# A hybrid encoder layer on one core: the next head's decay mask queued behind the old head's last power, the first product's place fixed between the x tiles, and the first feed-forward products taken chunk by chunk

## The chip, the core and the metric

The kernel runs on one core of a Trainium2 chip. The core has a matrix engine (TensorE, PE in the profile; its weight loads are PEld), a vector engine (VectorE, DVE), an activation engine (ScalarE, ACT), a general engine (GpSimd, POOL) and a queue that issues transfers (SyncE, SP). Each has its own instruction queue and works through it in order; semaphores join them. The metric is the device time of one execution in microseconds (us), lower is better. A difference of the medians below 0.2% can't be told from no change.

## What is computed

One layer of a streaming encoder, on 1024 new frames of one stream and 64 next frames of another, 1088 tokens in all, width 1024:

```
z  = x @ w_in                                  # 1024 -> 8200 columns
A: GLU -> causal depthwise conv, width 31 -> LayerNorm -> swish -> @ w_a_out
B: 4 heads of a matrix memory, in chunks, gated with exp(d - m) below the diagonal
   h = num / max(|den|, exp(-m)); per-head norm (h - mu) * rsqrt(var + eps); sigmoid gate -> @ w_b_out
merged = sigmoid(g_A) * y_A + sigmoid(g_B) * y_B
x1 = LayerNorm(alpha * x + merged @ w_out)
x2 = LayerNorm(alpha * x1 + relu(x1 @ w_ff1)^2 @ w_ff2)       # hidden width 4096
```

All data are float32. Outputs are the two streams' x2 and the new states.

## The kernel before

**Products.** The 1088 tokens stand in three chunks of 384, 384 and 320 columns (`CHUNKS`), features on the 128 partitions. To keep float32 accuracy, every operand is split in a high part, rounded by ScalarE, and a low part, the difference, taken by VectorE (`split`, L339 and L342), and a product is three matmuls: high by high (L331), high by low (L334), low by high (L335), in `mm3`. A *unit* (`unit`) is 128 output features: eight k steps of three matmuls for each of three chunks, 72 matmuls, then a `post` function for each chunk, which evicts the PSUM tile. After each chunk `slot` advances background work by a step: the heads (`mlstm`), the convolution on VectorE (L572), and a third queue, misc, that holds the gates, the spilling of x and the norms. A unit's weights are loaded two units ahead (`wload`) and split one unit ahead (`wsplit`).

**Order.** A scheduler puts the instructions of each engine in order: those traced first have priority, but one whose operands its own model takes as ready may pass one that is not. `pin` sets an instruction behind the one traced before it on its engine; what comes after it may still pass. `tc.issue_after(i)` puts all that a block traces on the engine of `i` behind `i` in that engine's queue.

**Start.** x comes in nine tiles of 128 rows (`load_x`, L157, four buffers). `trans_x` transposes a tile on TensorE in two halves (L169), ScalarE takes the high part (L171), VectorE the low part (L172). Chunk 0 consists of tiles 0 to 2. Three tiles are asked for first, then the first weights, the fourth tile and the second weights. The first product, unit 0 on chunk 0, is traced after tile 2 and kept in `early` until its unit takes it. The gates (`gates`) ask for a few small transfers as well (L224, L225, L228).

**Heads.** Each of the four heads runs over nine chunks of 128 tokens. Chunk 8 is the second stream. At a chunk's end VectorE takes statistics of the head's output `isb` (L519 to L524), GpSimd computes the inverse root by an addition and a power (L525, L526), VectorE applies it (L527, L528), and TensorE transposes the result (L450) a step later. `head_decay` makes the next head's mask `dt`: GpSimd broadcasts a row (L391), fills (L392) and selects the part below the diagonal (L393), ScalarE takes nine exponentials (L395). `dt` has one buffer, so this can start when the old head has read its last mask (L478).

**First norm and feed-forward.** `out_proj` makes merged @ w_out chunk by chunk, eight products each, and starts `ln1` of a chunk when the chunk is done. `ln1` runs in the slots that follow: a split of the sum; then the mean over features (matmuls L697, L698), centred and squared data (L705, L707); then the variance (L716, L719) and a power; then the scale spread over the partitions (L730, L731), and `finish`, which leaves chunk `ci` of x1 as `X1H`, `X1L`, two feature blocks at a time (L820, L339, L342). The triple `waits` says how many slots pass ahead of the second, third and fourth of these steps. Then `first_units` takes the first two feed-forward units, each on chunks 0 and 1, then the third unit on chunks 0 and 1, kept in `early`, then both on chunk 2. The third unit's weights are the first in the pool `whl2`, whose space comes free at the end of `out_proj`. From there blocks of the feed-forward follow, in a seven-product scheme (`wino_pair`), then the last block and the second norm.

Of the kernel before, what the change touches and what calls it, by code (L numbers as in the profile page):

```python
# [20 lines left out]
T = SP + SS  # L21
P = 128
# [27 lines left out]
def hybrid_layer(ctx, tc, x_prompt, x_sample, cache_conv, state_C, state_n, state_m, w_in, b_gate,  # L50
# [36 lines left out]
    def gtile():  # L87
        return pools["psg"].tile([P, 512], F32, tag="m", name="g")
# [66 lines left out]
    def load_x(i):  # L155
        xt = xp.tile([P, D], F32, tag="x", name="x")
        nc.sync.dma_start(xt[:tile_len(i)], xrows(i))  # L157
        return xt

    def trans_x(i, xt):  # L160
        ci, off, n = i // 3, (i % 3) * P, tile_len(i)
        if i % 3 == 0:
            XH.append(ph.tile([P, KT, CN], F32R, tag="p", name="xh"))
            XL.append(pl.tile([P, KT, CN], F32R, tag="p", name="xl"))
        for kh in range(2):
            ps = mtile().rearrange("p (k t) -> p k t", k=4)
            for k in range(4):
                kk = kh * 4 + k
                TE.transpose(ps[:, k, :n], xt[:n, kk * P:(kk + 1) * P], ident[:n, :n])  # L169
            hi = XH[ci][:, kh * 4:kh * 4 + 4, off:off + n]  # L170
            S.activation(hi, ps[:, :, :n], AF.Copy)  # L171
            V.tensor_tensor(XL[ci][:, kh * 4:kh * 4 + 4, off:off + n], ps[:, :, :n], hi.bitcast(F32), ALU.subtract)  # L172

    xt0 = [load_x(0), load_x(1), load_x(2)]

    def start_x():
        for i in range(4):
            trans_x(i, xt0[i])
            if i == 1:
                wsplit(0, True)  # L180
            if i == 2:
                early[0] = product(*his[0], 0)
        for i in range(4, NT):
            trans_x(i, load_x(i))
        vp = xp.tile([NV, D], F32, tag="x", name="vp")
        nc.sync.dma_start(vp[0:CW, :], w_dw[0])
        for r, src in ((R_BDW, b_dw), (R_AG, ln_a_g), (R_AB, ln_a_b), (R_HN, hn_g), (R_G1, ln1_g), (R_B1, ln1_b)):
            nc.sync.dma_start(vp[r:r + 1, :], src[0:1, :])
        nc.sync.dma_start(vp[R_SN:R_SN + 1, :], state_n[0, 0].rearrange("h k -> (h k)")[None, :])
        cp = xp.tile([CB, D], F32, tag="x", name="cp")  # L190
        nc.sync.dma_start(cp, cache_conv[0, 0])
        ps = mtile()
        for k in range(KT):
            TE.transpose(ps[:, k * NV:(k + 1) * NV], vp[:, k * P:(k + 1) * P], ident[:NV, :NV])
        V.tensor_copy(vecs, ps[:, :KT * NV].rearrange("p (k v) -> p k v", k=KT))
        ps = mtile()
        for k in range(KT):
            TE.transpose(ps[:, k * CB:(k + 1) * CB], cp[:, k * P:(k + 1) * P], ident[:CB, :CB])
        V.tensor_copy(cacheT, ps[:, :KT * CB].rearrange("p (k v) -> p k v", k=KT))
# [115 lines left out]
    def product(hi, lo, ci):  # L315
        n = CHUNKS[ci][1]
        ps = gtile()
        for k in range(KT):
            mm3(ps[:, :n], hi[:, k, :], lo[:, k, :], XO["h"][ci][:, k, :n], XO["l"][ci][:, k, :n], k == 0, k == KT - 1)
        return ps  # L320

    def unit(hi, lo, post, chunks=(0, 1, 2)):
        for ci in chunks:
            ps = early.pop(ci) if ci in early else product(hi, lo, ci)
            while later:
                later.pop()()
            post(ci, *CHUNKS[ci], ps)
            slot()

    def mm3(out, lh, ll, rh, rl, start, stop, pinned=False, more=False):  # L330
        first = TE.matmul(out, lh, rh, start=start, stop=False, skip_group_check=more)  # L331
        if pinned:
            pin(first)
        TE.matmul(out, lh, rl, start=False, stop=False, skip_group_check=more)  # L334
        TE.matmul(out, ll, rh, start=False, stop=stop, skip_group_check=more)  # L335
# [39 lines left out]
    def head_start(h):  # L375
# [10 lines left out]
            G.memset(t[SS:, 8, :HD].bitcast(F32), 0.0)  # L386
        HT["vh"], HT["vl"] = vh, vl

    def head_decay(h):
        dt = pools["hd"].tile([P, NT, P], F32, tag="dt", name="dt")  # L390
        G.partition_broadcast(dt.rearrange("p c t -> p (c t)")[:, :T], negM[32 * h:32 * h + 1, :])  # L391
        G.memset(dt[:, 8, SS:], MASKED)  # L392
        G.affine_select(dt, dt, [[0, NT], [1, P]], ALU.is_ge, MASKED, base=0, channel_multiplier=-1)  # L393
        for c in range(NT):
            S.activation(dt[:, c, :], dt[:, c, :], AF.Exp, bias=ucol[:, c, h:h + 1])  # L395
        HT["dt"] = dt
# [29 lines left out]
    def mlstm(h):  # L426
# [30 lines left out]
        for c in range(NT):  # L457
# [65 lines left out]
            V.bn_aggr(st[:n, 10:12], st[:n, 4:10])  # L523
            V.tensor_scalar(st[:n, 2:3], st[:n, 11:12], st[:n, 1:2], st[:n, 1:2], ALU.mult, ALU.mult)  # L524
            G.tensor_scalar(st[:n, 3:4], st[:n, 2:3], EPS, None, ALU.add)  # L525
            G.tensor_tensor(st[:n, 12:13], st[:n, 3:4], mhalf[:n], ALU.pow)  # L526
            V.tensor_tensor(st[:n, 13:14], st[:n, 12:13], st[:n, 1:2], ALU.mult)  # L527
            V.tensor_scalar(isb[:n, :HD], isb[:n, :HD], st[:n, 10:11], st[:n, 13:14], ALU.subtract, ALU.mult)  # L528
            yield
# [286 lines left out]
    def ln1(ci):  # L816
        n = CHUNKS[ci][1]

        def finish(k, z):
            S.activation(z, z, AF.Identity, scale=vecs[:, k, R_G1:R_G1 + 1], bias=vecs[:, k, R_B1:R_B1 + 1])  # L820
            if k % 2:
                ks = slice(k - 1, k + 1)
                split(X1H[ci][:, ks, :n], X1L[ci][:, ks, :n], Y2[ci][:, ks, :n])
        X1H.append(ph.tile([P, KT, CN], F32R, tag="p", name="x1h"))
        X1L.append(pl.tile([P, KT, CN], F32R, tag="p", name="x1l"))

        def square():
            return pools["lnq" if ci == 2 else "ln1"].tile([P, 4, CN], F32, tag="sq", name="sq")
        yield from ln_feature(Y2[ci], n, pools["ln1"], square, finish, ((2, 3, 2), (2, 3, 2), (1, 2, 1))[ci], YS[ci])
        if ci == 2:  # L830
            lnq.close()
            lns.close()
            pools["hw0"] = pool("hw0", 1, stack=win)
# [166 lines left out]

    def first_units(kh, hi, lo):
        post = post_r(0, kh, True)
        unit(hi, lo, post, (0, 1))
        held.append((hi, lo, post))
        if kh == 1:
            pools["whl"] = pools["whl2"]
            third = 2 + next(i for i, p in enumerate(pieces) if p[3] == 1)
            wsplit(third)
            for ci in range(2):
                early[ci] = product(*his[third], ci)  # L1010
            drain("misc")
            for h in held:
                unit(*h, (2,))
            whs.close()
            pools["hw1"] = pool("hw1", 1, stack=win)
# [115 lines left out]
    def wload(i):  # L1131
        if i < len(pieces) and i not in raws:
            ap = pieces[i][0]
            raws[i] = wpool.tile([P, KT * P], F32, tag="wr", name="wr")
            nc.sync.dma_start(raws[i].rearrange("p (k n) -> p k n", n=int(ap.shape[2])), ap)
# [17 lines left out]

    idx = 0
    wload(0)
    xt0.append(load_x(3))
    wload(1)
    for ap, fn, kind, _ in jobs:
        if ap is None:
            fn()  # L1160
# [37 lines left out]
```

## Time and profile before

| | |
|---|---|
| timed runs before (3) | 1964.35, 1967.43, 1967.94 us; median 1967.43 |
| the profiled execution's own time | 1964.53 us |
| its span, first to last instruction | 1962.7 us |
| TensorE busy | 1930.5 us, 98% |
| VectorE, ScalarE, GpSimd busy | 1389.7 (71%), 637.7 (32%), 123.0 us (6%) |
| mean granted TensorE clock | 0.993 of full |
| bytes moved | 131.06 MB, mean 67 GB/s |

The profile is of one execution. A row of the timeline has the start, the length, the engine, the line, the operation, what is written and read, the count of merged instructions, and in brackets the idle time of the engine ahead of it with what ended it. A row of waits has the total idle time, the number of waits and the longest. A row of a table by stretches has the stretch, its length, then for PE, PEld, DVE, ACT and POOL the busy time and the number of instructions, the granted TensorE clock, the share of the 16 transfer engines and GB/s. Matmuls overlap, so a matmul's length is about twice the time from its start to the next one's.

### The profile page before, as it was taken

To read this page: it belongs to the slowest core of one execution; us is meant where nothing else is said; L and a number is where in the kernel's file an instruction comes from. 1 tells how busy PE (TensorE), PEld (TensorE's weight loads), DVE (VectorE), ACT (ScalarE), POOL (GpSimd) and SP (SyncE) were. 2 spreads that over 40 slices of the span, in tenths; PEclk is the share of its full clock that TensorE was granted. 3 is DMA by queue.
4 is the path that set the end of the run, shared out by engine and by line. 5 is a ranking of instruction groups with operands and counts; after the bars stand their busy time and mean duration, and the time that the engine had idled before them with its cause. 6 is when DMAs were issued, how large, how long until landed. Compare 5 with 4: busy or idle time off the path is not lost.

```text
span 1962.7 us, 30510 instructions
## 1 busy us (share of the span) xinstructions
PE 1930.5 (98%) x12396; PEld 1908.2 (97%) x12396; DVE 1389.7 (71%) x2735; ACT 637.7 (32%) x1203; POOL 123.0 (6%) x229
## 2 busy tenths in 40 slices
PE   8999999999999999999999998999999999999998
PEld 7999999999999999999999998999999999999996
DVE  3957876787678777887774547767685858577647
ACT  3323322332233223323352214523233332414232
POOL 1112210001000100000000000000000000000005
PEclk9999999999999999999999999999999999999999
DMA  4122311121212221225334211011111111111212
GB/s 152 37 82 54 120 49 55 54 71 48 62 35 65 64 66 34 65 89 181 119 107 146 91 39 39 22 54 33 54 44 54 44 44 55 44 55 34 75 44 91
DMA packets 171745, 131.06 MB, mean 67 GB/s; under 512 B 8272, under 2 KB 166464, under 8 KB 171604
## 3 DMA queue, kind: packets, MB, share of 16 engines
q1 hardware_dynamic: 171603, 129.11, 21.7%
q8 instruction: 97, 1.59, 0.3%
q14 instruction: 45, 0.36, 0.1%
HBM read 104.39 MB, written 24.63 MB: 66 GB/s over the span
## 4 chain that ended last, share of the span: by engine, by line
PE 91%; DVE 5%; issue 2%; POOL 1%; ACT 1%; DMA 0%; SPq 0%; DVEq 0%; POOLq 0%; ACTq 0%
PE g L331 28%; PE g L334 28%; PE g L335 28%; PE m L331 1%; PE m L335 1%; PE m L334 1%; DVE acc L572 1%; PE m L466 0%; PE m L1068 0%; PE m L413 0%; PE m L472 0%; DVE wl L342 0%; PE m L450 0%; DVE isb L528 0%; DVE C L504 0%
## 5 line engine op out<-in xcount | busy, mean ns | idle before, releaser
L331 PE MATMUL g<-xh,wh 128*128 128x384 f32 (+1 forms) x1920 | 636.0, 331 | 0.0
L334 PE MATMUL g<-xl,wh 128*128 128x384 f32 (+1 forms) x1920 | 630.8, 329 | 0.0
L335 PE MATMUL g<-xh,wl 128*128 128x384 f32 (+1 forms) x1920 | 629.8, 328 | 0.0
L334 PEld LDWEIGHTS g<-xl,wh 128*128 128x128 f32 x1920 | 362.6, 189 | 0.3
L331 PEld LDWEIGHTS g<-xh,wh 128*128 128x128 f32 x1920 | 362.5, 189 | 0.2
L335 PEld LDWEIGHTS g<-xh,wl 128*128 128x128 f32 x1920 | 362.2, 189 | 0.0
L572 DVE SCALAR_TENSOR_TENSOR acc<-glu,vecs,acc 128x1118 f32<-128x1118 f32 x240 | 331.4, 1381 | 3.5
L339 ACT ACTIVATE wh<-wr 128x1024 fp32r<-128x1024 f32 (+1 forms) x168 | 166.0, 988 | 458.4 <-PE g L334 363.6
L342 DVE TENSOR_TENSOR wl<-wr,wh 128x1024 fp32r<-128x1024 f32 (+1 forms) x168 | 191.1, 1138 | 113.6 <-ACT wh L339 110.8
L334 PE MATMUL g<-x1l,wh 128*128 128x384 f32 (+1 forms) x768 | 253.5, 330 | 1.6 <-DVE x1l L342 1.5
L331 PE MATMUL g<-x1h,wh 128*128 128x384 f32 (+1 forms) x768 | 254.3, 331 | 0.1
L335 PE MATMUL g<-x1h,wl 128*128 128x384 f32 (+1 forms) x768 | 253.0, 329 | 0.0
L334 PE MATMUL g<-hvl,wh 128*128 128x272 f32 x784 | 223.4, 287 | 0.0
L331 PE MATMUL g<-hvh,wh 128*128 128x272 f32 x784 | 221.3, 290 | 0.5 <-DVE y L981 0.5
L335 PE MATMUL g<-hvh,wl 128*128 128x272 f32 x784 | 221.6, 288 | 0.0
L983 DVE TENSOR_TENSOR y<-g,y 128x272 f32<-128x272 f32 (+1 forms) x540 | 156.6, 338 | 26.9 <-PE g L335 25.1
L331 PEld LDWEIGHTS g<-hvh,wh 128*128 128x128 f32 x784 | 145.8, 189 | 2.6 <-DVE y L983 1.3
L334 PEld LDWEIGHTS g<-x1l,wh 128*128 128x128 f32 x768 | 145.1, 189 | 2.4 <-DVE x1l L342 2.4
L334 PEld LDWEIGHTS g<-hvl,wh 128*128 128x128 f32 x784 | 147.3, 188 | 0.0
L335 PEld LDWEIGHTS g<-hvh,wl 128*128 128x128 f32 x784 | 146.4, 188 | 0.0
L331 PEld LDWEIGHTS g<-x1h,wh 128*128 128x128 f32 x768 | 145.1, 189 | 0.6 <-ACT x1h L339 0.5
L335 PEld LDWEIGHTS g<-x1h,wl 128*128 128x128 f32 x768 | 145.0, 189 | 0.0
(276 smaller groups left out, 2360.5 us busy)
## 6 DMA issues: line engine op xcount, KB each, us to landing
wr<-in_w_in_dram SPq DMA_DIRECT2D x64, 512.0 KB
wr<-in_w_ff_dram SPq DMA_DIRECT2D x64, 512.0 KB
x<-in_x_prompt_dram SPq DMA_DIRECT2D x8, 512.0 KB
dwT<-acc SPq DMA_DIRECT2D x8, 512.0 KB
wr<-in_w_b_out_dram SPq DMA_DIRECT2D x8, 512.0 KB
wr<-in_w_a_out_dram SPq DMA_DIRECT2D x8, 512.0 KB
wr<-in_w_out_dram SPq DMA_DIRECT2D x8, 512.0 KB
out_dram<-o SPq DMA_DIRECT2D x16, 256.0 KB
```

The costliest lines, as they stand in the source:

```text
L331: first = TE.matmul(out, lh, rh, start=start, stop=False, skip_group_check=more)
L334: TE.matmul(out, lh, rl, start=False, stop=False, skip_group_check=more)
L335: TE.matmul(out, ll, rh, start=False, stop=stop, skip_group_check=more)
L339: a = S.activation(hi, src, AF.Copy)
L342: V.tensor_tensor(lo, src, hi.bitcast(F32), ALU.subtract)
L572: V.scalar_tensor_tensor(acc, glu[:, j:j + AC], vecs[:, c, j:j + 1], acc, ALU.mult, ALU.add))
L983: V.tensor_tensor(y, ps[:, pslc], y, ALU.add)
```

## The change

Four edits. At the start, the first weights are asked for ahead of the first four tiles of x; the first product is pinned behind tile 3's transposes, tile 4's transposes stand pinned between its two halves of four k steps, tile 5's behind it, and the second weights are traced after tile 5's load. At the heads, the broadcast for the next head's mask is queued on GpSimd behind the last power traced so far, which is the old head's last one. In the first norm, chunk 1's steps pass (1, 3, 1) slots instead of (2, 3, 2). At the start of the feed-forward, the two first units are taken on chunk 0, then the third unit on chunk 0, then the two on chunk 1, the third on chunk 1, and then the two on chunk 2. The added test in `unit` keeps the kept products for the unit that takes all three chunks.

```diff
-    def trans_x(i, xt):
+    def trans_x(i, xt, pinned=False):
@@
-                TE.transpose(ps[:, k, :n], xt[:n, kk * P:(kk + 1) * P], ident[:n, :n])
+                t = TE.transpose(ps[:, k, :n], xt[:n, kk * P:(kk + 1) * P], ident[:n, :n])
+                if pinned and kk == 0:
+                    pin(t)
@@
-    xt0 = [load_x(0), load_x(1), load_x(2)]
+    xt0 = []
 
     def start_x():
-        for i in range(4):
+        for i in range(3):
             trans_x(i, xt0[i])
             if i == 1:
                 wsplit(0, True)
-            if i == 2:
-                early[0] = product(*his[0], 0)
-        for i in range(4, NT):
+        trans_x(3, xt0[3], True)
+        hi, lo = his[0]
+        ps = gtile()
+        for k in range(KT):
+            if k == KT // 2:
+                trans_x(4, load_x(4), True)
+            mm3(ps[:, :CN], hi[:, k, :], lo[:, k, :], XH[0][:, k, :], XL[0][:, k, :], k == 0, k == KT - 1, k % 4 == 0)
+        early[0] = ps
+        x5 = load_x(5)
+        wload(1)
+        trans_x(5, x5, True)
+        for i in range(6, NT):
             trans_x(i, load_x(i))
@@ unit
-            ps = early.pop(ci) if ci in early else product(hi, lo, ci)
+            ps = early.pop(ci) if ci in early and len(chunks) == 3 else product(hi, lo, ci)
@@ head_decay
-        G.partition_broadcast(dt.rearrange("p c t -> p (c t)")[:, :T], negM[32 * h:32 * h + 1, :])
+        with tc.issue_after(root[0].ins) if root[0] else ExitStack():
+            G.partition_broadcast(dt.rearrange("p c t -> p (c t)")[:, :T], negM[32 * h:32 * h + 1, :])
@@ mlstm
-            G.tensor_tensor(st[:n, 12:13], st[:n, 3:4], mhalf[:n], ALU.pow)
+            root[0] = G.tensor_tensor(st[:n, 12:13], st[:n, 3:4], mhalf[:n], ALU.pow)
@@ ln1
-        yield from ln_feature(Y2[ci], n, pools["ln1"], square, finish, ((2, 3, 2), (2, 3, 2), (1, 2, 1))[ci], YS[ci])
+        yield from ln_feature(Y2[ci], n, pools["ln1"], square, finish, ((2, 3, 2), (1, 3, 1), (1, 2, 1))[ci], YS[ci])
@@ first_units
-        unit(hi, lo, post, (0, 1))
+        unit(hi, lo, post, (0,))
         held.append((hi, lo, post))
         if kh == 1:
             pools["whl"] = pools["whl2"]
             third = 2 + next(i for i, p in enumerate(pieces) if p[3] == 1)
             wsplit(third)
-            for ci in range(2):
-                early[ci] = product(*his[third], ci)
+            early[0] = product(*his[third], 0)
+            for h in held:
+                unit(*h, (1,))
+            early[1] = product(*his[third], 1)
             drain("misc")
             for h in held:
                 unit(*h, (2,))
@@ start of the loop over jobs
     wload(0)
-    xt0.append(load_x(3))
-    wload(1)
+    for i in range(4):
+        xt0.append(load_x(i))
```

More of the change, by code (lines that the diff above doesn't have):

```diff
@@ L387, in head_start @@
         HT["vh"], HT["vl"] = vh, vl
+    root = [None]
     def head_decay(h):
         dt = pools["hd"].tile([P, NT, P], F32, tag="dt", name="dt")
-        G.partition_broadcast(dt.rearrange("p c t -> p (c t)")[:, :T], negM[32 * h:32 * h + 1, :])
+        with tc.issue_after(root[0].ins) if root[0] else ExitStack():
+            G.partition_broadcast(dt.rearrange("p c t -> p (c t)")[:, :T], negM[32 * h:32 * h + 1, :])
         G.memset(dt[:, 8, SS:], MASKED)
```

## The prediction

> **What bounds the kernel now.** I read the page first, then the list of TensorE's waits, then a table by stretches of the span round each wait.
>
> ```profile
> span 1962.7 us, 30510 instructions
> PE 1930.5 (98%) x12396; PEld 1908.2 (97%) x12396; DVE 1389.7 (71%) x2735; ACT 637.7 (32%) x1203; POOL 123.0 (6%) x229
> ...
> PE m L169 <- DMA x<-in_x_prompt_dram: 8.5, 3, 4.4
> PE m L450 <- DVE isb L528: 6.7, 3, 2.3
> PE m L716 <- ACT sh L339: 2.9, 1, 2.9
> PE g L334 <- DVE x1l L342: 1.5, 2, 1.0
> ```
>
> TensorE sets the time: busy 98%, and no other engine comes near. What can be won without removing products is its idle time. Four groups of waits hold nearly all of it: at the start (L169, loads of x), at the end of the heads (L450, one wait each for heads 0, 1 and 2), and at the end of the first norm (L716, L334). The change touches these three places. Behind them stands a second loss, in the clock column (the last three columns are granted clock, DMA share, GB/s):
>
> ```profile
> 10.90:17.80 6.90, 4.82 (x19) 4.40 (x20) 4.07 (x6) 3.23 (x6) 0.00 (x0) 0.51 0.99 321
> 254.00:258.00 4.00, 1.82 (x11) 1.43 (x11) 2.45 (x4) 1.00 (x1) 3.75 (x11) 1.00 0.30 93
> 464.00:480.00 16.00, 16.00 (x88) 16.00 (x89) 13.99 (x16) 3.70 (x10) 0.00 (x0) 0.89 0.01 3
> 672.00:690.00 18.00, 18.00 (x100) 18.00 (x100) 15.95 (x18) 3.59 (x9) 0.00 (x0) 0.91 0.10 26
> 1223.00:1231.00 8.00, 8.00 (x32) 8.00 (x33) 1.60 (x4) 0.52 (x1) 0.85 (x1) 0.59 0.14 47
> ```
>
> After the second and third head waits and after the norm's wait TensorE runs at half clock for a while, busy all through. Lost: 16 x 0.11 = 1.8, 18 x 0.09 = 1.6 and 8 x 0.41 = 3.3 us. After the first head's wait it does not.
>
> **The change part by part: heads.** The end of head 1, VectorE and GpSimd in order of time, with an ordinary chunk before it:
>
> ```profile
> 438.33 0.27 DVE L524 TENSOR_SCALAR st<-st 128x1 f32<-128x1 f32 x1
> 439.80 0.41 DVE L528 TENSOR_SCALAR isb<-isb,st 128x256 f32<-128x256 f32 x1
> ...
> 450.91 1.36 POOL L391 PARTITION_BROADCAST dt<-negM  x1 [6.08 <-DVE C L504]
> 452.43 0.26 DVE L524 TENSOR_SCALAR st<-st 64x1 f32<-64x1 f32 x1
> 459.51 1.22 DVE L342 TENSOR_TENSOR wl<-wr,wh 128x1024 fp32r<-128x1024 f32 x1 [6.81 <-ACT wh L339]
> 459.65 1.18 POOL L525 TENSOR_SCALAR st<-st 64x1 f32<-64x1 f32 x1 [6.67 <-issue]
> 461.38 0.59 POOL L526 TENSOR_TENSOR st<-st,mhalf 64x1 f32<-64x1 f32 x1
> 462.15 1.22 POOL L393 TENSOR_SCALAR_AFFINE_SELECT dt<-dt 128x1152 f32<-128x1152 f32 x1
> 462.19 1.32 DVE L528 TENSOR_SCALAR isb<-isb,st 64x256 f32<-64x256 f32 x1
> 463.40 2.74 ACT L395 ACTIVATE dt<-dt,cols 128x128 f32<-128x128 f32 x9 [2.31 <-POOL dt L393]
> ```
>
> In an ordinary chunk L528 ends 1.9 us after L524 starts. Here it ends 11.1 us after: the next head's broadcast went first, and 6.67 us of GpSimd follow in which nothing is recorded ("issue") before the addition L525 runs. With the broadcast queued behind the power, L525 to L528 keep their ordinary pace and isb is ready at about 454.4, against 463.51 now. Even if VectorE still takes the weight split at 459.51 first, L528 ends at 459.51 + 1.22 + 0.6 = 461.3, two us before it does now. The waits of 6.7 us go (bounds 6.7, and 6.0 in that second order), and with them the two half-clock stretches, 3.4 us. I take **10.1**.
>
> What now stands behind the power on GpSimd: code change, broadcast, mask selection L393, then on ScalarE the nine exponentials L395. The broadcast starts about 6.1 us (the idle time before it above) after L526 ends at 453.6, so 459.7; with 1.36, the fill L392 and 1.22 the mask is done at 462.5, and now it ends at 463.37. No later, so ScalarE is held no longer. The unrecorded 7 us move too, in front of the next arithmetic on GpSimd:
>
> ```profile
> 502.01 0.12 POOL L540 MEMSET glu<- 128x30 f32 x1 [38.64 <-DVE acc L572]
> 570.97 0.27 POOL L525 TENSOR_SCALAR st<-st 128x1 f32<-128x1 f32 x1 [68.84 <-DVE st L524]
> ```
>
> GpSimd stands idle for 68.84 us there, ample cover. If it were not hidden it would cost 6.67 at a power again, the present 2.3 us wait. The spills of x (L367), still running at the end of head 0, are delayed by some 7 us, and SP's queue with them; the weights queued behind them are for the unit after the next, three products of up to 4.2 us away. The Trainium skill, GPSIMD Engine Reference, 2.1 Instruction dispatch, says the first call of a freshly loaded kernel pays a load of about 6 us with no visible instruction; the rows agree (6.67 and 6.08). By that rule the change removes no load, it only moves them, and the sum stays as it is.
>
> **Start.** SP's queue, TensorE, and the two engines that feed the first product:
>
> ```profile
> 4.19 3.58 SPq L224 DMA_DIRECT2D fa<-in_w_in_dram  x1
> 10.68 2.65 SPq L157 DMA_DIRECT2D x<-in_x_prompt_dram  x4
> 13.87 1.96 SPq L228 DMA_DIRECT2D smc<-in_state_m_dram  x4
> ...
> 4.37 4.53 PE L169 MATMUL m<-ident,x 128*128 128x128 f32 x24 [4.37 <-DMA x<-in_x_prompt_dram]
> 11.03 1.94 PE L169 MATMUL m<-ident,x 128*128 128x128 f32 x8 [2.13 <-DMA x<-in_x_prompt_dram]
> 14.92 0.66 PE L169 MATMUL m<-ident,x 128*128 128x128 f32 x2 [1.95 <-DMA x<-in_x_prompt_dram]
> 15.23 0.67 PE L331 MATMUL g<-xh,wh 128*128 128x384 f32 x1
> 20.93 3.27 PE L169 MATMUL m<-ident,x 128*128 128x128 f32 x28
> ...
> 11.70 2.63 DVE L172 TENSOR_TENSOR xl<-m,xh 128x512 fp32r<-128x512 f32 x4
> ```
>
> Now x tile 3's transposes end at 12.97 and the operands are there by 13.0 (the first two of the four at 11.70), but the product waits behind tile 4, which lands at 14.9. After the change the first weights lead the queue. The four loads of x and the weights take 11.03 - 4.37 = 6.7 us from first to last landing, 1.65 each, so TensorE starts 1.6 us later, at 6.0; tile 3 still lands fifth, near 11. The product starts at about 13.1, half of it passes, then come tile 4's eight transposes and the other half. Now product and tile 4 are done at 20.93 + 4 x 0.117 = 21.4. Then: with the gaps of 2.13 and 1.95 gone the clock may be full, 13.1 + 4.2 + 0.9 = 18.3 (24 matmuls at 0.175, eight transposes at 0.117); at the half clock of this stretch, 13.1 + 3.8 + 1.9 + 2.1 = 20.9. If the four state loads (1.96 on SP) also pass tile 4, it lands at 16.9 and the end is 19.9 at full clock, 22.7 at half. So between 3.1 won and 1.3 lost; I take **2**, since the transposes follow one another nearly without gaps from 6.0 on. The second weights stay unpinned and are ready at once, so I expect SP to issue them ahead of tile 4 as before.
>
> **Norm's end.** The four products of the first two feed-forward units, and what follows:
>
> ```profile
> 1202.33 0.34 PE L730 MATMUL m<-sh,ones 128*128 128x384 f32 x1
> 1202.68 0.34 PE L331 MATMUL g<-x1h,wh 128*128 128x384 f32 x1
> 1206.86 0.31 PE L697 MATMUL m<-sh,mean 128*128 128x320 f32 x1
> 1212.37 1.23 DVE L342 TENSOR_TENSOR wl<-wr,wh 128x1024 fp32r<-128x1024 f32 x1 [0.59 <-ACT wh L339]
> 1222.79 0.37 PE L716 MATMUL m<-mean,sh 128*128 128x2 f32 x1 [2.88 <-ACT sh L339]
> 1230.82 0.31 PE L730 MATMUL m<-sh,ones 128*128 128x320 f32 x1
> 1234.17 0.83 DVE L342 TENSOR_TENSOR x1l<-y,x1h 128x640 fp32r<-128x640 f32 x1
> 1239.48 0.83 DVE L342 TENSOR_TENSOR x1l<-y,x1h 128x640 fp32r<-128x640 f32 x1 [0.50 <-ACT x1h L339]
> ```
>
> A product takes 1206.86 - 1202.68 = 4.18 us. From L730 of chunk 1 to L730 of chunk 2 are 28.5 us for four products (16.7) and some 1.3 us of norm matmuls: 10.5 are lost, idle or half clock (the norm's ten at 0.1 to 0.17 each). Afterwards chunk 1's norm steps stand one and two slots earlier in the output projection, and chunk 1 is first read after three products of chunk 0 instead of one, 8.4 us later. All the chunk-1 waits should go; L716 of chunk 2 stands behind four products instead of three and loses the stalls ahead of it, so its 2.88 and the half clock go as well. New: between chunk 2's L730 and the first product on chunk 2 stands one product, not two. Its low parts come 4.2 to 9.5 us after L730 (1235.0 to 1240.31), while the product on 320 columns starts at 4.5 (0.35 for L730 and L731, 4.18 for the one product) and would have done three quarters of its 3.5 us (4.18 x 320/384) when it asks for the last of them: TensorE waits up to 9.5 - 4.5 - 2.6 = 2.4 us. I take 2 for it, and 0.5 for the earlier L716 of chunk 1, which finds VectorE busy. Net **8.0**; bounds 10.5 (no new wait) and 3 (the third unit's weights, split at 1212.37 to 1213.6, are wanted from about 1211: 2.6, with chunk 2's wait 2.4 and a half-clock stretch 1.7 to 3).
>
> **Sum.** 10.1 + 2 + 8.0 = 20 us off the profiled execution's 1964.5 (span 1962.7): 1944.5. The three timed runs before have a median of 1967.4, 2.9 above the profiled one. I put the time at **1945**, near the profiled basis, since waits that may or may not draw a half-clock stretch are what goes.
>
> **Rivals.** (1) The norm's end wins little, as at the bound of 3: it then gives 3 and not 8, 1949.5, or nothing, 1952.5. For it: VectorE and ScalarE are nearly full from 1203 on; against: they get 7 us more lead. (2) The half clock is not due to the head waits: then the heads give 6.7 and the time is 1948. For it: the first head's wait of 2.3 us left the clock at 1.00; against: 0.89 and 0.91 directly after the other two. By the Trainium skill, TensorE: Matmul & The Clock Gate, What's actually happening, half rate comes after an idle window of about 3.4 us, longer than these waits, which would speak for this rival; the trace shows half clock after 2.3 us, so the measurement decides. (3) The change does not do what it says: the scheduler keeps its order at the heads through another queue (VectorE still behind a late split), and only start and norm pay: 1954. (4) Slower: the exponentials L395 are queued on ScalarE ahead of the evictions that follow the head's last chunk. ScalarE then stands from about where the broadcast starts now, 450.9, until 462.5 + 2.74 = 465.2, 14.3 us. Of the three PSUM buffers one is still being read when that begins, so two products, 8.4 us, are covered. TensorE stops for 5.9 us and loses 1.7 to 3.4 more to the clock: 7.6 to 9.3 for each of three heads, 23 to 28 in all, giving 1967.5 to 1972.5, say 1970. It turns slower than before from 20 / 3 = 6.7 per head. Against: the mask selection ends no later than now, and now the exponentials stand behind the evictions.
>
> **How the numbers follow.** Forecast (1939 to 1950) 0.70; rival 1 0.12; rival 2 0.04; rival 3 0.06; rival 4 0.04; something that cancels most of it, within 0.2% of before, 0.04. Less than 0.2% (3.9 us) cannot be told from no change here. Faster: 0.70 + 0.12 + 0.04 + 0.06 = 0.92, less 0.02 for their upper ends, 0.90; same 0.06; slower 0.04. The range: all three parts at their good end, 10.1 + 3.1 + 10.5 = 23.7, so 1940.8, and 1.8 for scatter, 1939; at the other side rivals 1 and 3 on the basis of the median, 1956. Left out: some 0.12.
>
> **What would show it.** Heads right: no wait of L450 on L528, L525 within 1 us of L524 at each head's end, broadcast after L526, clock 1.00 at 464 and 672; wrong: L450 or another wait of 2 us there, or ScalarE idle before L395 for over 5 us with TensorE waiting. Start right: the first L331 near 13 and the last of the product with tile 4 by 20; wrong: a wait for x in its middle. Norm right: no wait at L716, a wait of about 2 us at chunk 2's L334 instead; wrong: waits at the third unit's L335 on wl. The whole is wrong if TensorE's idle time falls and the time does not.

## The result and the profile after

The changed kernel takes 1945.8 us (median of four runs, 1944.61 to 1947.92), the kernel before on the same chip 1967.5 (four runs, 1964.35 to 1967.94). The ratio is 0.9894, with an interval of 0.9877 to 0.9911: 17.5 to 24.2 us less. The forecast was 1945. The profiled execution took 1945.67 us, with a span of 1943.9. Of the kernel with chunk 1's slots back, below, one execution of five (2565.99 us, granted clock 0.685 against 0.998 in the others) is left out of every figure.

The page of the changed kernel, its first lines, and then its list of TensorE's waits (total, number, longest):

```profile
span 1943.9 us, 30514 instructions
PE 1922.5 (99%) x12396; PEld 1902.4 (98%) x12396; DVE 1390.9 (72%) x2735; ACT 638.1 (33%) x1204; POOL 124.0 (6%) x229
...
PE m L169 <- DMA x<-in_x_prompt_dram: 6.9, 1, 6.9
PE g L342 <- DVE y L995: 1.5, 2, 1.2
...
PE g L345 <- DVE xl L174: 0.9, 1, 0.9
PE m L744 <- ACT sh L350: 0.8, 1, 0.8
```

The three waits for isb (6.7 us before) are gone from the list, and so are the norm's 2.9 and 1.5. Three loads' waits (8.5 us) have become one of 6.9. One wait has grown: for y at L995 (L981 before), which stood at 0.5. Two are new: for xl (0.9), and for sh at L744 (0.8). Line numbers of the changed kernel are up to 16 higher than before.

For the gain by stages, the same three matmuls in both timelines will do as marks: the gates' transposes, the last head's last transposes, and the first transposes of the second norm. The timeline of the kernel before, and then that of the changed kernel:

```profile
76.17 1.17 PE L308 MATMUL m<-ident,fa 128*128 128x128 f32 x9 [0.52 <-DMA fa<-fc]
870.56 0.34 PE L450 MATMUL m<-ident,isb 64*128 64x64 f32 x2
1851.81 1.04 PE L1068 MATMUL m<-ident,y 128*128 128x128 f32 x8
```

```profile
74.28 1.17 PE L319 MATMUL m<-ident,fa 128*128 128x128 f32 x9 [0.51 <-DMA fa<-fc]
858.67 0.34 PE L464 MATMUL m<-ident,isb 64*128 64x64 f32 x2
1832.59 1.04 PE L1084 MATMUL m<-ident,y 128*128 128x128 f32 x8
```

The start gives 76.17 - 74.28 = 1.9 us. From there to the last head it is 794.39 against 784.39: 10.0. From there to the second norm it is 981.25 against 973.92: 7.3. The rest takes 0.4 more. The same differences, worked out from the same three marks in every profile of this study (us; a part marked * holds the change's own edits of that stage and no others):

| kernel | start | heads | norm and feed-forward |
|---|---|---|---|
| before | 76.2 | 794.4 | 981.2 |
| after | 74.3 * | 784.4 * | 973.9 * |
| heads alone (e1) | 77.6 | 784.5 * | 981.3 |
| start alone (e2) | 74.1 * | 794.9 | 979.7 |
| norm alone (e3) | 77.2 | 796.3 | 972.4 * |
| broadcast by transfer (e6) | 78.0 | 786.8 | 981.3 |
| slots back (e4) | 76.3 * | 784.4 * | 975.4 |
| loads back (e5) | 75.5 | 784.4 * | 972.5 * |
| sums on GpSimd (e7) | 75.1 * | 784.4 * | 978.2 |
| split first (e8) | 74.2 | 784.4 * | 972.5 * |
| squares on ScalarE (e9) | 75.1 * | 784.4 * | 970.9 |
| start and squares (e11) | 74.0 | 784.4 * | 970.9 |

The start scatters by up to 2 us with the same code (74.1 to 76.3 with the change, 76.2 to 77.6 without; the 78.0 of e6 has a small transfer of its own there). Part of that is the clock: the profile with 76.3 (e4) has it at 0.91 from 30 to 50, 1.8 us, where the changed kernel has 1.00. The heads scatter hardly at all once their waits are gone.

The end of head 1 after, on VectorE, GpSimd and ScalarE:

```profile
448.36 0.27 DVE L538 TENSOR_SCALAR st<-st 64x1 f32<-64x1 f32 x1
449.80 0.41 DVE L542 TENSOR_SCALAR isb<-isb,st 64x256 f32<-64x256 f32 x1
455.91 2.02 DVE L353 TENSOR_TENSOR wl<-wr,wh 128x1024 fp32r<-128x1024 f32 x1 [1.31 <-ACT wh L350]
...
448.72 0.21 POOL L539 TENSOR_SCALAR st<-st 64x1 f32<-64x1 f32 x1 [0.74 <-DVE st L538]
449.02 0.56 POOL L540 TENSOR_TENSOR st<-st,mhalf 64x1 f32<-64x1 f32 x1
455.63 1.37 POOL L405 PARTITION_BROADCAST dt<-negM  x1 [6.06 <-issue]
457.08 1.94 POOL L407 TENSOR_SCALAR_AFFINE_SELECT dt<-dt 128x1152 f32<-128x1152 f32 x1
...
562.97 0.26 POOL L539 TENSOR_SCALAR st<-st 128x1 f32<-128x1 f32 x1 [68.82 <-DVE st L538]
...
459.05 2.75 ACT L409 ACTIVATE dt<-dt,cols 128x128 f32<-128x128 f32 x9 [1.54 <-POOL dt L407]
```

L538 to the end of L542 now takes 1.85 us, the pace of an ordinary chunk, where it took 11.1. The broadcast starts 6.05 us after the power's end. If the second unrecorded stretch is still there, it lies in GpSimd's idle time: the next addition, L539 at 562.97, has 68.82 us of idle time ahead of it and starts 0.11 us after its L538 ends (562.86).

### The profile page after: what moved, and what is told of

It is laid out like the page before. It is cut to its first block, busy times and chain, and to the rows that moved or that the text cites. A ratio compares the mean times of both kernels' runs of the same rounds, so it can differ in the third digit from the quotient of the medians.

```text
span 1943.9 us, 30514 instructions
## 1 busy us (share of the span) xinstructions
PE 1922.5 (99%) x12396; PEld 1902.4 (98%) x12396; DVE 1390.9 (72%) x2735; ACT 638.1 (33%) x1204; POOL 124.0 (6%) x229
## 4 chain that ended last, share of the span: by engine, by line
PE 94%; DVE 4%; DMA 1%; ACT 0%; issue 0%; POOL 0%; DVEq 0%; SPq 0%; POOLq 0%; ACTq 0%
PE g L342 29%; PE g L345 29%; PE g L346 29%; PE m L342 1%; PE m L346 1%; PE m L345 1%; DVE acc L586 1%; PE m L480 0%; PE m L1084 0%; PE m L427 0%; DVE wl L353 0%; PE m L486 0%; PE m L464 0%; DMA x<-in_x_prompt_dram 0%; PE m L169 0%
## 5 line engine op out<-in xcount | busy, mean ns | idle before, releaser
L342 PE MATMUL g<-xh,wh 128*128 128x384 f32 (+1 forms) x1920 | 634.9, 331 | 0.0
L346 PE MATMUL g<-xh,wl 128*128 128x384 f32 (+1 forms) x1920 | 628.6, 327 | 0.0
L342 PEld LDWEIGHTS g<-xh,wh 128*128 128x128 f32 x1920 | 361.3, 188 | 0.7 <-ACT xh L173 0.3
L346 PEld LDWEIGHTS g<-xh,wl 128*128 128x128 f32 x1920 | 361.0, 188 | 0.1
L342 PE MATMUL g<-x1h,wh 128*128 128x384 f32 (+1 forms) x768 | 252.8, 330 | 0.0
L346 PE MATMUL g<-x1h,wl 128*128 128x384 f32 (+1 forms) x768 | 252.1, 328 | 0.0
L342 PE MATMUL g<-hvh,wh 128*128 128x272 f32 x784 | 221.8, 291 | 1.5 <-DVE y L995 1.5
L346 PE MATMUL g<-hvh,wl 128*128 128x272 f32 x784 | 222.4, 289 | 0.0
L342 PEld LDWEIGHTS g<-hvh,wh 128*128 128x128 f32 x784 | 146.5, 190 | 3.4 <-DVE y L995 1.9
L346 PEld LDWEIGHTS g<-hvh,wl 128*128 128x128 f32 x784 | 147.1, 189 | 0.0
L342 PEld LDWEIGHTS g<-x1h,wh 128*128 128x128 f32 x768 | 144.2, 188 | 0.1
L346 PEld LDWEIGHTS g<-x1h,wl 128*128 128x128 f32 x768 | 144.3, 188 | 0.0
```

## The experiments

All times are compared with runs of the kernel before on the same chip. The first four ran beside it at a median of 1966.31 us, the next four at 1965.21, the last three at 1966.89. The changed kernel's own runs stand beside the 1967.51 above, not beside these. So where a kernel differs from it by less than 0.2% (3.9 us) and the intervals of the two ratios overlap, the medians don't decide, and the text goes by the stages of the profiles, one execution each.

**The heads alone (e1).** To the kernel before is added only:

```diff
+    root = [None]
+        with tc.issue_after(root[0].ins) if root[0] else ExitStack():
+            G.partition_broadcast(...)
-            G.tensor_tensor(st[:n, 12:13], ...)
+            root[0] = G.tensor_tensor(st[:n, 12:13], ...)
```

> The kernel before with one edit of the change alone: the broadcast queued behind the old head's last power. Theory A (order: the waits of TensorE at the three heads and the half-clock stretches behind two of them both go): 10 us less than before, about 1957, the granted clock 1.00 in the 30 us after each head's end, no wait of L450 on isb. Rival (the half clock has another cause and stays): 6.7 us less, and 0.89 to 0.91 still recorded in two stretches. Rival (other edits of the change are needed for it): no gain.

Measured: 1955.65 us, 10.7 less; ratio 0.9943 (0.993 to 0.9957). The stage of the heads shrinks by 9.9 us, and no wait for isb is left. A table by stretches of this kernel (busy PE, PEld, DVE, ACT, POOL with counts, clock, DMA share, GB/s):

```profile
464.00:480.00 16.00, 16.00 (x100) 16.00 (x99) 14.57 (x14) 3.19 (x7) 0.00 (x0) 1.00 0.17 45
672.00:690.00 18.00, 18.00 (x112) 18.00 (x111) 14.69 (x14) 3.44 (x5) 0.00 (x0) 1.00 0.14 35
```

The clock is 1.00 in the stretches that stood at 0.89 and 0.91. The rival by which the half clock stays (6.7) is out: the half clock went with the waits.

**The start alone (e2).** The kernel before with `trans_x`, `start_x` and the load order of the change.

> The kernel before with the edits of the start alone (order of the first loads and the pins). Theory A: 2 us less than before, about 1965.5 against 1967.5; TensorE's first transposes near 6.9, the product with tile 4 done near 19. Rival (the later start eats what the pins win): no difference. The trace of after gives 1.9 by the place of the gates' first transposes.

Measured: 1962.66 us (11 runs), 3.7 less; ratio 0.9985 (0.9976 to 0.9994), that is 1.2 to 4.7 us. Its timeline on TensorE:

```profile
6.79 5.96 PE L169 MATMUL m<-ident,x 128*128 128x128 f32 x32 [6.79 <-DMA x<-in_x_prompt_dram]
...
18.91 3.32 PE L169 MATMUL m<-ident,x 128*128 128x128 f32 x28
```

Product and tile 4 are done at 18.9, against 21.4 before. Over the five profiles with this start and the three with the old one (the table's first column: 74.3, 74.1, 76.3, 75.1, 75.1; 76.2, 77.6, 77.2) the mean gain is 77.0 - 75.0 = 2.0. In the profiled execution a part of the gain isn't the start's: the norm's wait was 1.4 us where the kernel before shows 2.9, and the stage is 1.5 shorter with the same code. So 2 us from the start agree with all of it; the rival (no gain) is out by the interval, though 3.7 us is just under 0.2%.

**The norm's end alone (e3).** The kernel before with `first_units`, the added test in `unit` and chunk 1's (1, 3, 1).

> The kernel before with the edits of the norm's end alone (the slots of chunk 1, the units by chunks). Theory A: 7 to 8 us less than before, about 1960; no wait at L716 and no half clock near 1223 to 1231, a wait of about 1.5 at the first seven-product block and half clock for some 3 us behind it. Rival (the gain at this place comes from the earlier parts, which shift the work against it): under 3 us.

Measured: 1958.74 us, 7.6 less; ratio 0.996 (0.9947 to 0.9972). The stage is 8.8 us shorter here, 1.5 more than in the changed kernel. The expected half clock at the first seven-product block didn't come: TensorE is busy for 8.51 of 10 us there (1258 to 1268), as in the changed kernel, but at a clock of 1.00 and not 0.83. The three medians add up to 10.7 + 3.7 + 7.6 = 22 us against 21.7 for all edits together: no sign that the parts disturb one another.

This kernel keeps the old heads, so its three head waits can be laid beside those of the two others that have them. In the kernel before, half clock followed the second and the third wait, not the first. The stretches behind the three waits in the kernel with the start alone:

```profile
254.00:266.00 12.00, 10.30 (x54) 10.23 (x55) 9.95 (x12) 2.74 (x9) 5.61 (x11) 0.86 0.29 86
462.00:474.00 12.00, 10.54 (x64) 10.47 (x65) 11.44 (x14) 3.64 (x10) 1.22 (x1) 1.00 0.16 42
668.00:680.00 12.00, 10.13 (x52) 10.06 (x53) 10.08 (x12) 2.74 (x9) 1.60 (x3) 0.86 0.18 45
```

and in this one:

```profile
254.00:266.00 12.00, 9.53 (x47) 9.14 (x46) 8.62 (x10) 4.86 (x12) 7.38 (x13) 0.86 0.29 85
462.00:474.00 12.00, 9.73 (x48) 9.35 (x47) 8.81 (x10) 4.79 (x12) 2.73 (x7) 0.86 0.18 45
668.00:680.00 12.00, 9.73 (x49) 9.35 (x48) 8.30 (x10) 5.41 (x12) 3.33 (x7) 0.86 0.18 45
```

Nearly the same wait (2.2 to 2.5 us) is followed by a half clock (0.86 over 12 us, 1.7 us lost) in some executions and not in others: seven times of nine. That fits the 1.9 us that the heads take longer here than in the kernel before (796.3 against 794.4): three stretches of half clock, not two.

**The broadcast by a transfer (e6).** The kernel before; the order at the heads is left, the code change is taken away:

```diff
+        nc.sync.dma_start(nmD, negM[0:P:32])
-        G.partition_broadcast(dt.rearrange(...)[:, :T], negM[32 * h:32 * h + 1, :])
+        nc.sync.dma_start(dt.rearrange(...)[:, :T], nmD[h:h + 1, :].partition_broadcast(P))
```

> The kernel before, with the order of the heads kept and the code change taken away: the rows of the decay mask are written to DRAM once, and each head's mask is filled by a broadcasting transfer on SP's queue instead of the broadcast on GpSimd. Theory A refined (the late addition is late because the broadcast ahead of it brings some 7 us of unrecorded time on GpSimd before the next arithmetic): the addition L525 follows its L524 within 1 us although the mask's order is untouched, no wait of L450, 10 us less than before, about 1957. Rival B (it is the order on GpSimd itself, the mask's fill and selection ahead of the addition): the addition still runs several us late, and the gain is under 5 us. Rival C (the transfer waits at the head of SP's queue and holds up the weights behind it): new waits of TensorE on weights, slower than the kernel with the broadcast alone moved.

Measured: 1957.33 us, 9.0 less; ratio 0.9951 (0.9938 to 0.9963). GpSimd at the end of head 1, and VectorE's L526, which is L524 of the kernel before:

```profile
453.61 1.21 POOL L395 TENSOR_SCALAR_AFFINE_SELECT dt<-dt 128x1152 f32<-128x1152 f32 x1 [0.46 <-DMA dt<-nmD]
...
454.91 0.21 POOL L527 TENSOR_SCALAR st<-st 64x1 f32<-64x1 f32 x1
...
453.78 0.27 DVE L526 TENSOR_SCALAR st<-st 64x1 f32<-64x1 f32 x1
```

The addition starts 0.86 us after L526 ends, although the mask's selection still stands ahead of it: without the broadcast there are no 6.67 unrecorded us. So what made the addition late was the broadcast ahead of it; that it is a load of code, as the prediction reads it, no run here shows. The order itself is not free: GpSimd stops at the selection for 0.46 us until the transfer has landed, and the addition behind it starts 0.86 us after its L526 where the changed kernel has 0.09. TensorE waits 2.0 us for isb in this kernel, 1.6 of it at head 0. Most of the lateness there is not the order's: VectorE's step behind the power, L529, takes 1.64 us at head 0 and 0.15 at head 1, while GpSimd adds up x for its spills beside it. The list of waits, and head 0 on VectorE and GpSimd:

```profile
PE m L452 <- DVE isb L530: 2.0, 2, 1.6
```

```profile
248.76 1.64 DVE L529 TENSOR_TENSOR st<-st 64x1 f32<-64x1 f32 x1 [1.71 <-POOL st L528]
...
248.70 1.68 POOL L369 TENSOR_TENSOR xs<-xh,xl 128x320 f32<-128x320 f32 x2
```

The profile's stage of the heads is 7.6 us shorter against 9.9 with the broadcast moved, and a half clock follows the wait at head 0 (0.92 from 240 to 262). Theory A refined holds for the mechanism and was 1 to 2.5 us too good on the size; of rival B the 0.86 us remain, and of rival C nothing shows.

**Chunk 1's slots back (e4).**

```diff
-((2, 3, 2), (1, 3, 1), (1, 2, 1))[ci]
+((2, 3, 2), (2, 3, 2), (1, 2, 1))[ci]
```

> The changed kernel with chunk 1's slots back at (2, 3, 2), the order of the units by chunks kept. Theory A (both halves of the edit are needed: the order gives chunk 1 two products more, the slots give its steps two places more): chunk 1 of x1 comes two slots later, some 8 us, and TensorE waits for it at its first product: 3 to 6 us slower than the changed kernel, about 1949 to 1952. Rival (the order of the units alone does it): within 1 us of the changed kernel, 1945, and without the wait of 0.8 at L744.

Measured: 1948.8 us; ratio 0.9918 (0.9905 to 0.9932), 3.0 us above the changed kernel. The profile is of one more execution:

> The same kernel as e4_slots_back once more, for a profile: the 3 us that it is slower than the changed kernel stand by Theory A as a wait of TensorE at chunk 1's first products (DVE x1l or ACT x1h) or at chunk 1's norm steps; by the rival that chunk 2 pays (its steps follow chunk 1's two slots later) as a wait at L727 or L741 of chunk 2 or at chunk 2's product.

It took 1949.1. The timeline of TensorE in the norm's end:

```profile
1192.48 0.34 PE L744 MATMUL m<-sh,ones 128*128 128x384 f32 x1
...
1198.35 0.41 PE L712 MATMUL m<-sl,mean 128*128 128x320 f32 x1 [1.04 <-DVE sl L353]
1203.79 0.45 PE L346 MATMUL g<-x1h,wl 128*128 128x384 f32 x1 [0.51 <-DVE wl L353]
1212.93 0.27 PE L730 MATMUL m<-mean,sh 128*128 128x2 f32 x1 [0.85 <-ACT sh L350]
```

Chunk 1 (384 columns) is 8.3 us later than after the change (1184.21 there), 2.0 of it from the start, and TensorE doesn't wait for it: the three products on chunk 0 cover that. Chunk 2 (320 columns) pays 1.04 and 0.85. For the first, VectorE takes the low part of its sum at 1197.82, directly behind a low part of chunk 1 that it began at 1196.95; that the second has the same cause is likely, but not shown. The place is the rival's: chunk 2's norm steps, though at L712 and L730. The size is only in part Theory A's: of the 3.4 us between the two profiles 2.0 lie in the start, which is the same code, and 1.5 in this stage. Without the half clock that the changed kernel's execution had there (below), and this one had not, the stage's difference is 2.9. So by these profiles 5.8 us of the stage's gain come from the order of the units, and 1.5 to 3 more from the slots.

**The first loads back in their old order (e5).** Tiles 0, 1, 2, then the first weights, then tile 3; the pins stay.

> The changed kernel with the first loads in their old order (tiles 0, 1, 2, the first weights, tile 3), all pins kept. Theory A (the pins give the gain of the start, the order of the loads little, since five transfers have landed by 11 us in either order and the product waits for VectorE's low parts): within 1 us of the changed kernel; first transposes back at 4.4, gaps for x at 9 to 11, the product still near 13 to 14. Rival (the order gives it, by transposes without gaps and so full clock): 1.5 to 2.5 us slower than the changed kernel, half clock in the product.

Measured: 1945.41 us; ratio 0.9899 (0.9886 to 0.9913), no difference from the changed kernel. TensorE in the start:

```profile
4.36 5.35 PE L169 MATMUL m<-ident,x 128*128 128x128 f32 x24 [4.36 <-DMA x<-in_x_prompt_dram]
...
14.65 1.06 PE L169 MATMUL m<-ident,x 128*128 128x128 f32 x8 [0.35 <-DMA x<-in_x_prompt_dram]
21.60 0.43 PE L169 MATMUL m<-ident,x 64*128 64x64 f32 x4 [1.17 <-DMA x<-in_x_sample_dram]
```

The product is done 1.4 us earlier than in the changed kernel, and most of that is given back at once: the last tile lands late, 1.17. Behind this wait the clock drops, which it doesn't in the changed kernel, and takes another 1.7 us (4 x 0.43):

```profile
23.00:27.00 4.00, 4.00 (x15) 4.00 (x15) 0.48 (x2) 0.21 (x1) 0.00 (x0) 0.57 0.08 29
```

Up to 23 the clock is 1.00, so the rival's half clock in the product did not come. The gain of the start stands with the pins alone; the order of the loads shows no worth.

**The first weights split first (e8).**

```diff
+        wsplit(0)
         for i in range(3):
             trans_x(i, xt0[i])
-            if i == 1:
-                wsplit(0, True)
@@ behind tile 5's load
+        with tc.issue_after(a3.ins):
+            wsplit(1)
```

> The changed kernel with the first weights' split ahead of tile 0's (they lead the queue, so they have landed by then) and the second weights' split held behind tile 3's. Theory on the gap of 1.4 us at 12.6 (VectorE takes the weights' low part, 1.23, between tiles 1 and 2, so tile 2's low part is late for the product): the gap goes, 1.0 to 1.4 us faster than the changed kernel, about 1944.6. Rival (the tiles' landing sets it): no difference, the product's second matmul still near 14.0.

Measured: 1944.03 us; ratio 0.9895 (0.9879 to 0.991). The gap of 1.4 us at the product is gone, but the first transposes come at 7.37 instead of 6.86, and the ninth tile is done at the same time: the stage ends at 74.2, against 74.3 in the changed kernel. What the profile gains (span 1942.5 against 1943.9) lies in the stage of the norm, whose code is the same. There the seven-product scheme starts with the same gaps in both; in the changed kernel, and then in this one:

```profile
1246.00:1256.00 10.00, 8.51 (x54) 8.07 (x53) 8.38 (x27) 1.86 (x4) 0.00 (x0) 0.83 0.16 53
```

```profile
1246.00:1256.00 10.00, 8.51 (x66) 8.03 (x65) 9.54 (x32) 1.77 (x4) 0.00 (x0) 1.00 0.18 53
```

TensorE is busy for 8.51 of 10 us in both, but one execution has the clock at 0.83 and the other at 1.00. The stages differ by 1.4 us, all of the 1.4 in the spans. It tells nothing of the split, so its worth stays unsettled, within the scatter of the start.

**Sums on GpSimd (e7).** For the first four weight tiles of the seven-product scheme all four sums (L959 to L962) go to GpSimd:

```diff
+        nv[0] += 1
+        E = G if nv[0] <= 4 else V
-        V.tensor_tensor(c[3], c[2], c[3], ALU.add)
+        E.tensor_tensor(c[3], c[2], c[3], ALU.add)
...
```

> The changed kernel with one addition: the four sums over each of the first four seven-product weight tiles (L959 to L962) run on GpSimd instead of VectorE. The theory on the 2.1 us of gaps and the half clock at 1246 to 1253 (VectorE, full from 1230 to 1246, delivers the first updates of y, L995, late): VectorE is relieved of 3.3 us ahead of 1249, the gaps and the half clock go, 2 to 3.5 us faster than the changed kernel, about 1942.5. Rival (GpSimd takes the sums so slowly that the weights' low parts come late, or TensorE waits there for another thing): no gain, or a new wait on wl, up to 3 us slower.

Measured: 1951.56 us; ratio 0.9929 (0.9917 to 0.9941), 5.8 above the changed kernel: worse than the rival. Here are the three engines of this kernel:

```profile
1239.26 0.99 POOL L965 TENSOR_TENSOR wr<-wr 128x256 f32<-128x256 f32 x1
...
1239.58 1.10 DVE L941 TENSOR_TENSOR t<-r,t 128x384 f32<-128x384 f32 x1
...
1241.30 1.06 ACT L350 ACTIVATE wh<-wr 128x1024 fp32r<-128x1024 f32 x1 [2.28 <-POOL wr L966]
```

The four sums take 3.6 us in a row. ScalarE stands for 2.28 us at the split that needs them, and every high part queued behind it is late: TensorE then waits 1.9 us for one (hvh). A subtraction of VectorE that runs beside the sums takes 1.10 us, and the next one 1.09; in the changed kernel they take 0.55 each (the first of them here):

```profile
1239.44 0.55 DVE L941 TENSOR_TENSOR t<-r,t 128x384 f32<-128x384 f32 x1
```

By the Trainium skill, GPSIMD Engine Reference, 8. Key points, GpSimd shares its interfaces to the memory with VectorE and the two contend where VectorE reads two operands from it; these rows agree.

**Squares on ScalarE (e9).** Six calls of the third and fourth unit:

```diff
+            sq[0] += kt
+            if kt == 1 and sq[0] <= 6:
+                S.activation(d, d, AF.Square)
+            else:
                 V.scalar_tensor_tensor(d, p, 0.0, d, ALU.max, ALU.mult)
```

> The changed kernel, the squares of the third and fourth feed-forward units (six calls of L927) taken by ScalarE as a Square instead of by VectorE. The theory on the gaps at 1246.6 and 1248.8 (VectorE, full from 1230 to 1246, updates y late), which the sums on GpSimd couldn't test because ScalarE and VectorE then waited for GpSimd: 3.1 us less on VectorE, on an engine with 6 us free there, so the gaps go, 1.5 to 1.7 us faster than the changed kernel, and up to 3.3 where that one had the half clock: about 1943. Rival (ScalarE becomes the late one, since its queue then holds two steps for each tile): the gaps stay or move to a wait on hvh, no gain or up to 2 us slower.

Measured: 1943.63 us (1942.42 to 1944.19); ratio 0.9881 (0.9864 to 0.9897), 2.2 less than the changed kernel, with intervals that overlap. The table by stretches of this kernel, with the first of the two rows of the changed kernel below it:

```profile
1230.00:1246.00 16.00, 16.00 (x105) 15.79 (x104) 14.77 (x35) 12.62 (x31) 0.00 (x0) 1.00 0.10 34
1246.00:1256.00 10.00, 10.00 (x79) 9.75 (x78) 9.32 (x30) 1.40 (x2) 0.00 (x0) 1.00 0.17 53
```

```profile
1230.00:1246.00 16.00, 16.00 (x109) 16.00 (x108) 15.89 (x37) 9.67 (x23) 0.00 (x0) 1.00 0.10 34
```

VectorE goes from 15.89 to 14.77 us busy of 16, and ScalarE from 9.67 to 12.62. The gaps are gone: TensorE is busy for 10.00 of 10, and the stage is 1.6 us shorter than in the kernels with the gaps and full clock (970.9 against 972.5), 3.1 shorter than in the changed kernel's execution with half clock. The cause named for them, a full VectorE, is borne out: 3 us of work less on it, and they are gone. The rival, a wait on ScalarE's hvh, doesn't show.

**Both (e11).** The same, with the loads in their old order, `pool("xp", 5)` in place of 4, and the gates' small loads behind the tiles.

> As the last one, and the start with the old order of the first loads, five buffers for x instead of four, and the gates' small transfers asked for behind the x tiles' (their weights in a place of their own). Theory on the start (after the pins the last tile's landing sets the end of the stage, 1.2 us of wait for x_sample where the product ended 1.35 us earlier): the tiles land earlier, the wait goes, 1 to 1.5 us faster than with the squares alone, about 1942. Rival (the small transfers, now later, hold up the gates' matmuls near 29): no gain, a wait at L243 or at the bias.

Measured: 1942.96 us (1942.54 to 1943.24); ratio 0.9878 (0.9863 to 0.9893). It has the lowest median of the study, and all its runs lie below all runs of both the kernel before and the changed one. Against the squares alone the 0.7 is no gain that can be told. The wait for the last tile is gone and another took its place:

```profile
20.77 1.05 PE L170 MATMUL m<-ident,x 128*128 128x128 f32 x8 [1.60 <-DVE xl L175]
```

TensorE now waits for VectorE's low parts (1.60). The rival's wait for the gates' weights doesn't show.

## Why the prediction was right

The forecast was 20 us off the profiled execution, 10.1 + 2 + 8.0; the profiles show 10.0 + 1.9 + 7.3, less 0.4. By the medians it is 21.7, with the interval given above. The sum was near, and its terms were near, but two of them came about in part in another way than forecast.

**Heads, 10.1: right in every step.** The waits and the half clock went. The broadcast came 6.05 us behind the power (6.1 in the prediction), and ScalarE stood only 1.54 us ahead of the exponentials. The step "in front of the next arithmetic, ample cover" held at head 1 (68.82 us). The selection took 1.94 instead of 1.22, beside a split of VectorE that took 2.02 where the prediction's row has 1.22. At head 0 the unrecorded time (6.81 us) stood ahead of two spills, and the selection ran behind them at 262.51, 10.9 us behind its broadcast; TensorE was busy for 22.00 of the 22 us from 240 on. The reading of the 6.67 us as the broadcast's doing was only argued in the prediction; the kernel without the broadcast shows it. That it is a load of code stays a reading.

**Start, 2: right in size, with one step off.** TensorE began at 6.86, not at 6.0: the four loads ran behind the weights, and the landing of the first was mis-sized by 0.9. The 32 transposes then took 5.74 us without a gap, and the product's second matmul waited 0.94 us for VectorE, which the prediction did not have. Against that the clock was full, and product and tile 4 were done at 19.0, inside the 18.3 to 20.9. The second weights did stay ahead of tile 4 on SP's queue. Crediting the order of the loads with full clock was idle: with the old order and the pins the clock is full up to 23 and the time is the same.

**Norm's end, 8.0 forecast, 7.3 measured: two terms failed and nearly cancel.** The step that failed first is the new wait: "TensorE waits up to 2.4 us", taken as 2, at chunk 2's product. None came. TensorE and VectorE of the changed kernel there:

```profile
1217.91 0.31 PE L342 MATMUL g<-x1h,wh 128*128 128x320 f32 x1
...
1218.94 0.31 PE L345 MATMUL g<-x1l,wh 128*128 128x320 f32 x1
1219.09 0.36 PE L342 MATMUL g<-x1h,wh 128*128 128x320 f32 x1
...
1222.06 0.83 DVE L353 TENSOR_TENSOR x1l<-y,x1h 128x640 fp32r<-128x640 f32 x1 [0.49 <-ACT x1h L350]
```

The last low parts are ready at 1222.89, as late as the prediction had them (9.5 us after L744 at 1213.40, the old L730). But from 1217.91 to there TensorE has run 33 matmuls without a gap (4.98 us at 0.15), and one product on this chunk has 24. So the two units' products on chunk 2 run interleaved (the L342 at 1219.09 stands ahead of the L346 of the step begun before it): as long as a low part is missing for one, the other has work. The prediction had costed a single product.

The second failure is that what follows was not looked at. The wait of 0.5 foreseen for chunk 1 came as 0.76, at L744 and not at L716's place. And 33 us behind chunk 2's spread of the scale, at the start of the seven-product scheme, TensorE idles for 1.5 us of 10 (0.5 in the kernel before) and in this execution runs at half clock for a while, 1.4 us by the comparison in the experiment with the first split. Added up afterwards: 10.5 lost before, less 0.76, 1.0 and 1.4, is 7.3, as measured. The 1.4 is this execution's luck: three more kernels of the study have the same 1.5 us of gaps and a full clock, and the one with the norm's edits alone gains 8.8. The bound of 3, by a late split of the third unit's weights, did not come in the changed kernel; with the slots back it shows as the 0.51 on wl.

**The rivals.** (1) The norm's end wins little: out, 7.3 here and 8.8 alone. Its argument read too much into ScalarE, which from 1202 to 1223 is busy for 14.41 of 21 us (VectorE 17.95). (2) The half clock has another cause than the head waits: out, since with the heads alone 9.9 us and a clock of 1.00 came. The reading that a head wait draws half clock was right, its price of 3.4 for two of three waits was that of one execution: 3.4 to 5.1 in the three that have these waits (two, two and three stretches of 1.7). (3) The change doesn't do what it says: out, L539 follows L538 at once. (4) The exponentials block ScalarE: out, it stood for 1.54 us ahead of them, and TensorE had no wait there.

**The basis.** The profiled execution was taken as the basis and not the median, 2.9 higher. The profiled executions differ by 18.9 and the medians by 21.7; the table by stages shows scatter of that size in the start and in the old kernel's half-clock stretches, but no profile of a run at the median shows where its 2.9 us lie. So the 1945, set near the lower basis, was met partly by luck: 20 us off the median would be 1947.4, still inside the range. The range's upper end of 1956 doesn't quite hold rival 3 on the basis of the median (1954 + 2.9).

## What to carry to other kernels

Where an engine shows several microseconds of idle time that nothing accounts for, look at what ran on it just before: an instruction that leaves such a stretch behind it belongs behind the short latency-critical ones, in front of the engine's longest idle time; taking the broadcast away altogether showed here that it was the cause. When a stage is tightened, go on to the stage that follows and ask which engine is nearly full there: the gain lost at the seven-product scheme was got back by moving 3 us of squares from VectorE to ScalarE, while moving sums to an idle GpSimd cost 5.8. And before pricing a wait on late operands, see whether another product stands in the queue that can run meanwhile.

## What the runs showed that was not expected

**Equal waits are followed by half clock in some executions and not in others.** Head waits of 2.2 to 2.5 us were in seven of nine cases, and the same gaps at the seven-product scheme in one execution (0.83) and not in four others (1.00: the norm alone, the slots back, the loads back, the first split). At the start the wait of 1.17 us with the loads back was (0.57), that of 1.60 in the kernel with both edits was not (1.00). So the length of a wait doesn't decide it alone; what else does, no run here shows. By the Trainium skill, TensorE: Matmul & The Clock Gate, What's actually happening, activity is judged in a window that runs freely, of about 3.4 us; that agrees with stretches that come and go with the same wait, though here no wait of 3.4 us was needed.

**An earlier mask costs ScalarE more.** In the kernel with the transfer the exponentials of head 0 start earlier and alternate with sigmoids, which need another table. From 225 to 280 its ScalarE loads a table five times, 1.28 us each, in the changed kernel once. From 230 to 280, which holds the nine exponentials in both, it is busy for 18.05 us, in the changed kernel for 14.22. Nobody waited for ScalarE here, so it cost nothing that shows.

**VectorE is slower beside GpSimd.** Beside GpSimd's sums VectorE's subtractions took 1.10 and 1.09 us in place of 0.55, and beside GpSimd's spills a step of 0.15 took 1.64. So work that goes to an idle GpSimd is paid in part by VectorE, and here, where VectorE was the full one, that took back part of what the move was to give.
